# Scale and shift of the normalised rows ahead of the feed-forward: on VectorE in pieces, in place of GpSimd

## The chip, the core and the metric

The kernel runs on one core of a Trainium2 chip. The metric is the device time of one execution in microseconds. The core's engines work side by side, each through its own queue in order: TensorE (PE; PEld is its weight load), VectorE (DVE), ScalarE (ACT), GpSimd (POOL), and SyncE (SP), whose queue starts the transfers (DMA).

## What is computed

A decoder trunk of two layers over 256 tokens of 2048 values, float32. Cut to what matters here, of each layer:

```python
mod = (silu(c) @ w_ada[l] + b_ada[l]).reshape(B, N_MOD, 1, D_MODEL)     # sh_m, sc_m, gt_m, sh_f, sc_f, gt_f
...                                                # attention and RWKV heads give mix
x = layer_norm(DEEPNORM_ALPHA * x + gt_m * mix, ln1_w[l], ln1_b[l])
u = x * (1 + sc_f) + sh_f
gate, up = jnp.split(u @ w_gate_up[l], 2, axis=-1)
ffn = (jax.nn.silu(gate) * up) @ w_down[l]
x = layer_norm(DEEPNORM_ALPHA * x + gt_f * ffn, ln2_w[l], ln2_b[l])
```

The first `layer_norm` ends with a scale by `ln1_w` and a shift by `ln1_b`. The change concerns these two operations.

## The kernel before

`channel` holds the second half of a layer. The rows after the output projection lie in `z` as two halves of 128 tokens with 2048 values each; `normalise` (L1069 to L1078) takes off the mean and divides by the deviation. From there two paths leave. On the first, `inputs` and `make_u` (L349 to L362) transpose `z` on TensorE in 128x128 blocks (L354, L1100), and ScalarE and VectorE make from each transposed column block the pair `u`, a rounded part and the remainder (L358, L360, L361; in layer 1 half of the blocks by L1105 to L1107). The scale and shift of the norm are folded into the factors `a` and `b` here, so that this path reads the unscaled `z`. On the second path `affine` (L1172 to L1181) multiplies `z` by `ln1_w` and adds `ln1_b`, in place, in 16 pairs of which each takes 512 columns of one half: 8 multiplications and 8 additions a layer, L1180 and L1181. Their result is read only when the down projection adds the residual (L1261). Since they write `z` in place, each has to come after the transposes that read its columns. The rows of `ln1_w` and `ln1_b` are loaded to all partitions (`lnw`, `lnb`, 1 MB each); the same two buffers are loaded again with `ln2_w` and `ln2_b` (L1233, L1235) once the last piece has read them.

The feed-forward goes through eleven gate steps f of 512 hidden columns. A gate step is one `stream` over 16 blocks of the contraction. For each block `steps` (L364 to L388) starts two transfers of 256 KB into `raw` (4 buffers), rounds them on ScalarE into `hi` (L380, 3 buffers), and takes the remainder on VectorE into `lo` (L381, 2 buffers); TensorE then runs 12 products of 128x512 (L402, L403, L405), of which L403 reads `lo`. Below, lo 8 and step 8 mean the eighth block of layer 0's first gate step.

Beside this a second stream computes the modulation `mod` from `w_ada`: a 512 KB transfer into `ast` (2 buffers) and one VectorE instruction into `aacc` (L257) for each part, about 1.1 per block while layer 0's first gate step runs and 0.75 after.

The order on each engine is not the order of the code: the Tile framework replays the program against its own timeline and places each instruction where it becomes ready there. The code's order sets only what may go before what. The same two operations stand behind the feed-forward for `ln2`, on VectorE already (L1275, L1276), between the u of the next layer.

Of the kernel before, what the change touches and what calls it, by code (L numbers as in the profile page):

```python
# [67 lines left out]
def hybrid_trunk_kernel(  # L68
# [8 lines left out]
    V, S, G, PE = nc.vector, nc.scalar, nc.gpsimd, nc.tensor  # L77
# [12 lines left out]
    def bank(name="mb", tag="mb"):  # L90

        if tag == "cb":
            return ps.tile([P, 512], F32, tag="cb", name=name)
        t = f"m{turn[0]}"
        turn[0] ^= turn[1]
        return ps.tile([P, 512], F32, tag=t, name=name, bufs=1)
# [293 lines left out]
    def stream(srcs, W, kts, lhs, pieces, banks, first=True, last=True, ts=(0, 1), room=None, held=None):  # L390


        kept = []
        for i, hi, lo in held or steps(srcs, W, kts, room):
            kept.append((i, hi, lo))
            lt = lhs[i]
            st, sp_ = first and i == 0, last and i == len(kts) - 1
            for t in ts:
                xh, xl = lt[:, 0, t * P:(t + 1) * P], lt[:, 1, t * P:(t + 1) * P]
                for q, (c0, w) in enumerate(pieces):  # L400
                    bt = banks[t][q][:, 0:w]
                    PE.matmul(bt, lhsT=xh, rhs=hi[:, c0:c0 + w], start=st, stop=False)  # L402
                    PE.matmul(bt, lhsT=xh, rhs=lo[:, c0:c0 + w], start=False, stop=False)  # L403
                for q, (c0, w) in enumerate(pieces):
                    PE.matmul(banks[t][q][:, 0:w], lhsT=xl, rhs=hi[:, c0:c0 + w], start=False, stop=sp_)  # L405
        return kept
# [21 lines left out]
    def all_banks(n, ts=(0, 1)):  # L428
        return {t: [next_bank() for _ in range(n)] for t in ts}
# [685 lines left out]
    def channel(l, ys, wa, fp):  # L1115
# [4 lines left out]
        def ht_tile():  # L1120
            return fp.tile([P, 2, 2 * T], F32R, tag="ht", name="ht", bufs=12)
# [18 lines left out]
        for o in (0, 512):  # L1140
            for t in range(2):
                zq = z[:, t, o:o + 512]
# [4 lines left out]
        for c0, w in ((1024, 512), (1536, 512)):  # L1147
# [7 lines left out]
            for ts in ((0,), (1,)) if apart else ((0, 1),):  # L1155
                if apart:
                    held = stream(src, w, kts[n:], ys[n:], pieces, bk, first=False, ts=ts, room=room_ht, held=held)
                for t in ts:
                    for q in range(nq):
                        o = c0 + q * 512  # L1160
                        zq = z[:, t, o:o + 512]
# [7 lines left out]
        parts = inputs(fp, z, l, "ln1_w", "ln1_b", l, 4, 3, us, SPLIT_F[l])  # L1169

        def affine():
            lw = fp.tile([P, D], F32, tag="lnw", name="lnw", bufs=2)  # L1172
            dma(lw, ln1_w[l:l + 1, :].to_broadcast([P, D]))
            lb = fp.tile([P, D], F32, tag="lnw", name="lnb", bufs=2)
            dma(lb, ln1_b[l:l + 1, :].to_broadcast([P, D]))
            for t in range(2):
                for q in range(4):
                    o = q * 512
                    zq = z[:, t, o:o + 512]
                    G.tensor_mul(zq, zq, lw[:, o:o + 512])  # L1180
                    G.tensor_add(zq, zq, lb[:, o:o + 512])  # L1181

        def finish(t):
            mv, rs = rstd(fp, stt[t])
# [11 lines left out]
        for lo_g, hi_g in ((0, 6), (6, 11)):  # L1196
            hts = []
            for f in range(lo_g, hi_g):
                def gu(rv, k0, m, f=f):
                    return [(rv[:, :, s * 512:(s + 1) * 512], wg[:, k0:k0 + m, s, f * 512:(f + 1) * 512]) for s in range(2)]  # L1200
                bk = all_banks(2)
                if f == 0:
                    held = None
                    for kts, ts in parts:
                        held = stream(gu, 1024, kts, us[kts[0]:], [(0, 512), (512, 512)], bk, kts[0] == 0, kts[-1] == KT - 1,
                                      ts, room_ht2 if ts == (0,) else None, held if ts == (1,) else None)
                    affine()
                    pace[0] = AF_[l]
                else:
                    stream(gu, 1024, list(range(KT)), us, [(0, 512), (512, 512)], bk)  # L1210
                hh = []
                for t in range(2):
                    sg = fp.tile([P, 512], F32, tag="sg", name="sg", bufs=2)
                    S.activation(sg, bk[t][0], AF.Silu)
                    V.tensor_mul(sg, sg, bk[t][1])
                    hh.append(sg)
                for k2 in range(2):
                    b = bank()
                    for i in range(2):
                        for t in range(2):  # L1220
                            PE.transpose(b[:, i * T + t * P:i * T + (t + 1) * P],  # L1221
                                         hh[t][:, (2 * k2 + i) * P:(2 * k2 + i + 1) * P], ident)
                    ht = ht_tile()
                    S.copy(ht[:, 0, :], b)
                    V.tensor_tensor(ht[:, 1, :], b, ht[:, 0, :].bitcast(F32), ALU.subtract)
                    for i in range(2):
                        hts.append(ht[:, :, i * T:(i + 1) * T])
            if first:
                gate_rows(gtf, l, 5)
            if not first:  # L1230
                stt = [fp.tile([P, 4, 6], F32, tag="bst", name="bst", bufs=2) for _ in range(2)]
                lw = fp.tile([P, D], F32, tag="lnw", name="lnw", bufs=2)
                dma(lw, ln2_w[l:l + 1, :].to_broadcast([P, D]))  # L1233
                lb = fp.tile([P, D], F32, tag="lnw", name="lnb", bufs=2)
                dma(lb, ln2_b[l:l + 1, :].to_broadcast([P, D]))  # L1235
            kts = list(range(4 * lo_g, 4 * hi_g))
            for c0, w in ((0, 1024), (1024, 512), (1536, 512)):
# [11 lines left out]
                for ts in ((0,), (1,)) if apart else ((0, 1),):  # L1249
# [5 lines left out]
                    for t in ts:  # L1255
                        for q in range(nq):
                            o = c0 + q * 512
                            zq = z[:, t, o:o + 512]
# [12 lines left out]
        for t in range(2):  # L1271
            for q in range(4):
                o = q * 512
                zq = z[:, t, o:o + 512]
# [73 lines left out]
```

## Time and profile before

| | |
|---|---|
| device time, median of 3 runs (lowest, highest) | 2716.19 us (2714.63, 2720.35) |
| profiled execution: device time, span of its core | 2716.41 us, 2714.6 us |
| busy share of TensorE, VectorE, ScalarE, GpSimd | 93%, 68%, 44%, 7% |
| transfers | 637.49 MB, mean 235 GB/s |
| L1180 and L1181 on GpSimd, 16 of each | 24.2 and 25.7 us |

A profile is read from the share of busy time to the stretches where the busiest engine waits: what it waits for there, and what that engine was doing. An instruction's row gives its start, its duration and, in brackets, how long its engine sat idle before it and what ended that. Where the row counts several instructions (x4), the duration is that of all.

### The profile page before, as it was taken

The numbers are of one execution on the slowest core, as the hardware profiler recorded it, in microseconds if no ns is written. First come the engines' busy times: TensorE is split into PE (matmuls) and PEld (weight loads), VectorE is DVE, ScalarE is ACT, GpSimd is POOL, SyncE is SP. The second block draws the span as 40 slices with busy tenths as digits, with TensorE's granted clock in tenths as the row PEclk, the third lists the DMA queues.
The fourth block names the chain that finished last, engine by engine and source line by source line (L and its number), as shares of the span: only waits on it lengthen the run. The fifth ranks groups of instructions, "written<-read, shape, count | busy, mean of one in ns | idle before, by whom it ended". The sixth has DMA issues, their size and how long they took to land. (4 is left out here: it accounts for less than half of the span.)

```text
span 2714.6 us, 41774 instructions
## 1 busy us (share of the span) xinstructions
PE 2517.3 (93%) x15325; PEld 2103.9 (78%) x15325; DVE 1853.5 (68%) x2437; ACT 1188.4 (44%) x2029; POOL 180.0 (7%) x387
## 2 busy tenths in 40 slices
PE   3789998797999999999999989989899999999998
PEld 2787886575788888888889877867788888888887
DVE  6877767879777777777788677565764545545456
ACT  2364452434444444444445544534444444344442
POOL 1002111003000000000000022110120000000000
PEclk9799997798999999999999999979999999999999
DMA  9968667597888888889888586423746655566654
GB/s 310 382 193 254 203 197 225 179 331 250 313 318 308 303 307 304 294 302 309 304 287 288 175 251 204 116 75 130 258 163 190 190 190 190 194 191 189 190 190 148
DMA packets 351999, 637.49 MB, mean 235 GB/s; under 512 B 75894, under 2 KB 142898, under 8 KB 350258
## 3 DMA queue, kind: packets, MB, share of 16 engines
q1 hardware_dynamic: 351794, 634.82, 71.1%
q8 instruction: 120, 1.97, 0.3%
q14 instruction: 85, 0.70, 0.1%
HBM read 622.08 MB, written 12.62 MB: 234 GB/s over the span
## 5 line engine op out<-in xcount | busy, mean ns | idle before, releaser
L380 ACT CAST hi<-raw 128x1024 fp32r<-128x1024 f32 (+2 forms) x728 | 757.8, 1044 | 1097.6 <-PE acc L405 810.6
L381 DVE TENSOR_TENSOR lo<-raw,hi 128x1024 fp32r<-128x1024 f32 (+2 forms) x728 | 885.9, 1220 | 515.8 <-PE acc L403 335.2
L403 PE MATMUL acc<-lo,u 128*128 128x512 f32 x1568 | 515.7, 396 | 16.9 <-DVE lo L381 16.6
L405 PE MATMUL acc<-hi,u 128*128 128x512 f32 x1568 | 507.3, 392 | 0.0
L257 DVE SCALAR_TENSOR_TENSOR aacc<-ast,cond,aacc 128x1024 f32<-128x1024 f32 x300 | 388.7, 1296 | 136.2 <-DMA ast<-in_w_ada_dram 135.1
L402 PE MATMUL acc<-hi,u 128*128 128x512 f32 x1568 | 459.7, 395 | 2.4 <-ACT u L360 1.1
L403 PEld LDWEIGHTS acc<-lo,u 128*128 128x128 f32 x1568 | 294.6, 189 | 83.9 <-DVE lo L381 23.7
L402 PEld LDWEIGHTS acc<-hi,u 128*128 128x128 f32 x1568 | 295.8, 189 | 65.4 <-ACT u L360 1.8
L405 PEld LDWEIGHTS acc<-hi,u 128*128 128x128 f32 x1568 | 296.4, 189 | 62.3 <-issue 0.7
L403 PE MATMUL acc<-lo,ht 128*128 128x512 f32 (+1 forms) x720 | 243.7, 377 | 2.7 <-DVE lo L381 2.6
L405 PE MATMUL acc<-hi,ht 128*128 128x512 f32 (+1 forms) x720 | 242.3, 375 | 0.0
L414 PE MATMUL acc<-u,hi 128*128 128x256 f32 x720 | 206.4, 293 | 12.9 <-ACT hi L380 12.9
L402 PE MATMUL acc<-hi,ht 128*128 128x512 f32 (+1 forms) x720 | 217.1, 376 | 0.0
L415 PE MATMUL acc<-u,hi 128*128 128x256 f32 x720 | 205.6, 292 | 0.0
L416 PE MATMUL acc<-u,lo 128*128 128x256 f32 x720 | 193.7, 295 | 5.3 <-DVE lo L381 5.3
L403 PEld LDWEIGHTS acc<-lo,ht 128*128 128x128 f32 x720 | 135.1, 188 | 28.8 <-DVE lo L381 5.2
L414 PEld LDWEIGHTS acc<-u,hi 128*128 128x128 f32 x720 | 142.8, 199 | 16.7 <-ACT hi L380 13.6
L405 PEld LDWEIGHTS acc<-hi,ht 128*128 128x128 f32 x720 | 135.6, 188 | 24.3
L402 PEld LDWEIGHTS acc<-hi,ht 128*128 128x128 f32 x720 | 134.8, 188 | 24.3
L415 PEld LDWEIGHTS acc<-u,hi 128*128 128x128 f32 x720 | 142.6, 198 | 3.5 <-issue 2.6
L416 PEld LDWEIGHTS acc<-u,lo 128*128 128x128 f32 x720 | 134.4, 198 | 9.5 <-DVE lo L381 6.9
L1067 POOL TENSOR_TENSOR brs<-brs,mhalf 128x1 f32<-128x1 f32 x8 | 5.2, 655 | 1637.3 <-DVE brs L1066 851.5
(349 smaller groups left out, 2950.9 us busy)
## 6 DMA issues: line engine op xcount, KB each, us to landing
ast<-in_w_ada_dram SPq DMA_DIRECT2D x368, 512.0 KB
raw<-in_w_gate_up_dram SPq DMA_DIRECT2D x704, 256.0 KB
raw<-in_w_down_dram SPq DMA_DIRECT2D x176, 512.0 KB
raw<-in_w_in_dram SPq DMA_DIRECT2D x82, 512.0 KB
raw<-in_w_out_dram SPq DMA_DIRECT2D x64, 512.0 KB
raw<-in_w_in_dram SPq DMA_DIRECT2D x120, 256.0 KB
ast<-in_w_ada_dram SPq DMA_DIRECT2D x32, 256.0 KB
lnw<-in_ln_w_dram SPq DMA_DIRECT2D x4, 1024.0 KB
```

The source lines that it names most:

```text
L257: ins = V.scalar_tensor_tensor(acc, t, cond[:, j:j + 1], acc, ALU.mult, ALU.add)
L380: S.copy(h, fl)
L381: ins = V.tensor_tensor(r, fl, h.bitcast(F32), ALU.subtract)
L402: PE.matmul(bt, lhsT=xh, rhs=hi[:, c0:c0 + w], start=st, stop=False)
L403: PE.matmul(bt, lhsT=xh, rhs=lo[:, c0:c0 + w], start=False, stop=False)
L405: PE.matmul(banks[t][q][:, 0:w], lhsT=xl, rhs=hi[:, c0:c0 + w], start=False, stop=sp_)
L414: PE.matmul(bt, lhsT=hi[:, c0:c0 + w], rhs=xh, start=st and opens, stop=False)
L415: PE.matmul(bt, lhsT=hi[:, c0:c0 + w], rhs=xl, start=False, stop=False)
L416: PE.matmul(bt, lhsT=lo[:, c0:c0 + w], rhs=xh, start=False, stop=sp_ and closes)
L1067: G.tensor_tensor(rs[:, 0:1], rs[:, 0:1], mhalf[:, 0:1], ALU.pow)
```

## The change

The multiplications and additions of `affine` are issued on VectorE. `affine` becomes a generator that hands control back after each pair; it is created after the first gate step, and two pairs are taken from it after the stream of each later gate step, so that in the code the last pair comes after the fifth gate step. Its two loads come with the first pair taken. Nothing else differs.

```diff
         def affine():
...
-                    G.tensor_mul(zq, zq, lw[:, o:o + 512])
-                    G.tensor_add(zq, zq, lb[:, o:o + 512])
+                    V.tensor_mul(zq, zq, lw[:, o:o + 512])
+                    V.tensor_add(zq, zq, lb[:, o:o + 512])
+                    yield
...
-                    affine()
+                    rows = affine()
                     pace[0] = AF_[l]
                 else:
                     stream(gu, 1024, list(range(KT)), us, [(0, 512), (512, 512)], bk)
+                    for _ in range(2):
+                        next(rows, None)
```

The framework does not leave the pieces where the code has them. In layer 0, VectorE's queue from the end of the normalisation (L1078) into the first gate step has this order before:

```order
L1078 TENSOR_SCALAR z<-z,brs 128x512 x2
L257 SCALAR_TENSOR_TENSOR aacc<-ast,cond,aacc 128x1024
L361 TENSOR_TENSOR u<-uf,u 128x256 x4
L381 TENSOR_TENSOR lo<-raw,hi 128x1024
L257 SCALAR_TENSOR_TENSOR aacc<-ast,cond,aacc 128x1024
L361 TENSOR_TENSOR u<-uf,u 128x256 x2
```

and, from the same place on, this one after the change (the multiplication is L1181 there and the addition L1182):

```order
L1078 TENSOR_SCALAR z<-z,brs 128x512 x2
L257 SCALAR_TENSOR_TENSOR aacc<-ast,cond,aacc 128x1024
L1181 TENSOR_TENSOR z<-z,lnw 128x512 x2
L361 TENSOR_TENSOR u<-uf,u 128x256
L1182 TENSOR_TENSOR z<-z,lnb 128x512 x2
L361 TENSOR_TENSOR u<-uf,u 128x256 x2
L381 TENSOR_TENSOR lo<-raw,hi 128x1024
L257 SCALAR_TENSOR_TENSOR aacc<-ast,cond,aacc 128x1024
L361 TENSOR_TENSOR u<-uf,u 128x256 x2
```

All 16 pieces stand among the u and lo of the first gate step, in four groups like this one, one for each 512 columns, as GpSimd's did; and a lo has up to three u and one aacc fewer ahead of it than before. Layer 1 has the same, among L1105, L1107 and L361.

In SyncE's queue the reload of the two buffers with the rows of ln2 has moved behind one more pair of weight transfers. This is the piece of the queue before:

```order
L372 DMA raw<-in_w_gate_up_dram 128x512 x2
L1233 DMA lnw<-in_ln_w_dram 128x2048
L253 DMA ast<-in_w_ada_dram 128x1024
L372 DMA raw<-in_w_gate_up_dram 128x512 x2
L1235 DMA lnb<-in_ln_b_dram 128x2048
```

and this is it after; the two loads are L1237 and L1239 there and wait for VectorE's last pieces:

```order
L372 DMA raw<-in_w_gate_up_dram 128x512 x2
L253 DMA ast<-in_w_ada_dram 128x1024
L372 DMA raw<-in_w_gate_up_dram 128x512 x2
L1237 DMA lnw<-in_ln_w_dram 128x2048
L253 DMA ast<-in_w_ada_dram 128x1024
L372 DMA raw<-in_w_gate_up_dram 128x512 x2
L1239 DMA lnb<-in_ln_b_dram 128x2048
```

The transfers are the same ones; the pair of weights for step 13 now starts ahead of `lnw`.

At one other place the order differs by more than single rows: in the attention of layer 1, VectorE takes the rotation of the queries (qr) and the end of a block inverse (tm, ytr) ahead of a softmax division and not behind it:

```order
+L757 TENSOR_TENSOR tm<-tm,m_17427 128x512
+L898 TENSOR_TENSOR qr<-ra,rb 128x5x32
+L899 TENSOR_TENSOR qr<-ra,rb 128x5x32
+L745 STREAM_TRANSPOSE ytr<-tm 128x512
+L898 TENSOR_TENSOR qr<-ra,rb 128x5x32
+L899 TENSOR_TENSOR qr<-ra,rb 128x5x32
 L948 TENSOR_TENSOR den<-den,es 128x8
 L949 RECIPROCAL den<-den 128x8
```

The six instructions stood behind the division (L954) before; the neighbouring parts of that attention block are shuffled likewise on TensorE and ScalarE.

## Rows read from the trace of the kernel before

**Rows 1.** The page's first part: busy time of each engine, share, count.

```profile
PE 2517.3 (93%) x15325; PEld 2103.9 (78%) x15325; DVE 1853.5 (68%) x2437; ACT 1188.4 (44%) x2029; POOL 180.0 (7%) x387
```

**Rows 2.** Stretches: length, busy per engine, clock, DMA share, GB/s.

```profile
core 0: us, PE busy (x) PEld busy (x) DVE busy (x) ACT busy (x) POOL busy (x), PEclk, DMA share, GB/s
...
640.00:700.00 60.00, 41.32 (x172) 32.49 (x173) 53.71 (x49) 29.67 (x61) 27.47 (x17) 0.83 0.66 210
...
700.00:750.00 50.00, 49.18 (x219) 39.65 (x218) 37.47 (x34) 22.30 (x25) 0.00 (x0) 1.00 0.94 330
...
sum 700.00, PE 694.70 PEld 572.85 DVE 529.64 ACT 308.50 POOL 0.00; mean PE 49.62 PEld 40.92 DVE 37.83 ACT 22.04 POOL 0.00
...
1425.00:1455.00 30.00, 29.41 (x234) 28.38 (x233) 28.18 (x43) 23.12 (x40) 0.00 (x0) 0.93 0.69 226
...
1975.00:1980.00 5.00, 5.00 (x25) 4.17 (x24) 4.88 (x11) 3.11 (x8) 2.71 (x2) 1.00 0.00 0
```

**Rows 3.** VectorE in order of time, layer 0's first gate step: start, duration, instruction.

```profile
651.96 5.71 DVE L361 TENSOR_TENSOR u<-uf,u 128x256 fp32r<-128x256 f32 x4
657.59 1.21 DVE L381 TENSOR_TENSOR lo<-raw,hi 128x1024 fp32r<-128x1024 f32 x1
658.73 1.27 DVE L257 SCALAR_TENSOR_TENSOR aacc<-ast,cond,aacc 128x1024 f32<-128x1024 f32 x1
659.92 2.94 DVE L361 TENSOR_TENSOR u<-uf,u 128x256 fp32r<-128x256 f32 x2
662.78 2.30 DVE L381 TENSOR_TENSOR lo<-raw,hi 128x1024 fp32r<-128x1024 f32 x1
...
667.24 0.75 DVE L361 TENSOR_TENSOR u<-uf,u 128x256 fp32r<-128x256 f32 x2
...
685.19 2.28 DVE L381 TENSOR_TENSOR lo<-raw,hi 128x1024 fp32r<-128x1024 f32 x1
```

**Rows 4.** GpSimd in order of time, same stretch, its last two pieces.

```profile
682.74 3.64 POOL L1181 TENSOR_TENSOR z<-z,lnb 128x512 f32<-128x512 f32 x2
```

**Rows 5.** GpSimd's first line of the pieces: shortest, median, longest in ns.

```profile
L1180 POOL TENSOR_TENSOR z<-z,lnw x16: 1263/1468/2264, 651.4 to 1999.5; 128x512 f32<-128x512 f32 x16
```

**Rows 6.** Waits by total, 636 to 760 us: us, times, longest.

```profile
PE acc L403 <- DVE lo L381: 8.6, 5, 4.3
POOL z L1180 <- PE mb L354: 8.0, 3, 3.9
```

**Rows 7.** TensorE in order of time, layer 0's first gate step.

```profile
687.52 0.74 PE L403 MATMUL acc<-lo,u 128*128 128x512 f32 x2 [4.25 <-DVE lo L381]
...
698.34 0.61 PE L403 MATMUL acc<-lo,u 128*128 128x512 f32 x2
...
701.06 0.61 PE L403 MATMUL acc<-lo,u 128*128 128x512 f32 x2
...
712.59 1.52 PE L402 MATMUL acc<-hi,u 128*128 128x512 f32 x6
```

**Rows 8.** VectorE at the same operation behind layer 0's feed-forward, in order of time.

```profile
1425.10 1.29 DVE L1275 TENSOR_TENSOR z<-z,lnw 128x512 f32<-128x512 f32 x2 [0.96 <-PE mb L354]
1426.31 0.42 DVE L361 TENSOR_TENSOR u<-uf,u 128x256 fp32r<-128x256 f32 x1
```

**Rows 9.** SyncE's queue of transfers in order of time, layer 0's first gate step.

```profile
687.54 0.81 SPq L372 DMA_DIRECT2D raw<-in_w_gate_up_dram  x2
...
692.84 0.63 SPq L1235 DMA_DIRECT2D lnb<-in_ln_b_dram  x1
```

**Rows 10.** ScalarE in order of time, layer 0's first gate step.

```profile
709.27 1.06 ACT L380 CAST hi<-raw 128x1024 fp32r<-128x1024 f32 x1 [1.47 <-DMA raw<-in_w_gate_up_dram]
```

**Rows 11.** ScalarE in order of time, start of layer 1's first gate step.

```profile
1962.38 1.04 ACT L380 CAST hi<-raw 128x1024 fp32r<-128x1024 f32 x1 [3.35 <-DMA raw<-in_w_gate_up_dram]
```

**Rows 12.** VectorE in order of time, attention of layer 1.

```profile
1823.48 0.17 DVE L948 TENSOR_TENSOR den<-den,es 128x8 f32<-128x8 f32 x1 [3.24 <-ACT pr L947]
...
1827.30 0.70 DVE L745 STREAM_TRANSPOSE ytr<-tm 128x512 f32<-128x512 f32 x1
```

## The prediction

> **What bounds the kernel now.** TensorE is busy for 93% of the span, VectorE for 68%, GpSimd for 7% [rows 1], so I looked first for stretches in which TensorE is not full. Around the work that the change moves there is one: in the 60 us from 640 on TensorE has 41.32 us at a mean clock of 0.83, VectorE 53.71 and GpSimd 27.47 [rows 2]. After 700 TensorE is full again: 694.70 of 700 us up to 1400, with the transfers at a share of 0.94 in the first 50 us [rows 2]. Whatever makes layer 0's first gate step end earlier is therefore carried on by a full TensorE; nothing behind it waits for a fixed time.
>
> VectorE in order of time comes next [rows 3]. From 651.96 up to lo 8 at 685.19 no row has an idle time: VectorE is the limit here, and TensorE waits 8.6 us for `lo` (once 4.25, at step 8) [rows 6, 7]. The rows also show two prices for one instruction. Two u in a row take 0.75 us where GpSimd is idle and 2.94 where it runs; a lo 1.21 and 2.30 [rows 3]. From start to start an undisturbed lo takes 1.14 and an aacc 1.19 (657.59, 658.73, 659.92), and a u 0.34 (half of 0.75, less the 0.07 by which each runs into the next); a stretched one of any size takes about 1.07 more, much the same for an instruction of 0.34 as for one of 1.19. That is a wait, not a slower pace: GpSimd's 16 pieces (the last two end at 686.38 [rows 4]) each hold up one VectorE instruction. I count 16 stretched instructions in this step of layer 0, 15 of them ahead of lo 8. The count can be checked: from 651.96 to lo 8 VectorE has 13 u, 5 lo and 6 aacc, 4.42 + 5.70 + 7.14 = 17.3 us, and 15 x 1.07 = 16.0; 651.96 + 33.3 = 685.3, and lo 8 starts at 685.19 [rows 3].
>
> GpSimd's instruction itself takes 1.263 us at best and up to 2.264 [rows 5], so the delay runs both ways. The Trainium skill (SBUF — State Buffer, Who interferes with whom) calls what the two engines share an exclusive lock: an instruction with two inputs in SBUF and a GpSimd instruction that reads SBUF exclude each other, and the later one waits for the whole of the first. By that rule a stretch could be as long as GpSimd's 1.263, and the removal worth 20.2 in place of the 17.1 below; the trace agrees in kind, and its 1.07 is what I use.
>
> **The change part by part, layer 0.** Removed: 16 stretches of 1.07 us, 17.1 us of VectorE's queue. Added: 16 instructions of 128x512. The trace has the same operation on VectorE behind the feed-forward: two in 1.21 us from start to start [rows 8], 0.605 each, so 9.7 us. The difference is 7.4 us up to the last u.
>
> The new order adds to it, since fewer u and aacc stand ahead of each lo. Walked with the same prices, VectorE has ahead of lo 8 now 10 u, 5 lo, 5 aacc and 12 pieces: 3.40 + 5.70 + 5.95 + 7.26 = 22.3, so lo 8 starts at 674.3, 10.9 earlier. From there to lo 12 come 4 lo, 6 u, 3 aacc and the last 4 pieces: 4.56 + 2.04 + 3.57 + 2.42 = 12.6; lo 12 ends at 688.0. TensorE begins L403 of step 12 at 701.06 now [rows 7]. It could follow: from step 8 at 675.4, four steps of 2.72 us (its spacing where it is full, 698.34 to 701.06 [rows 7]) bring it to 686.3. So step 12 starts 13.1 us earlier. The pieces' new wait, for the transposes that read their columns, I cost at nothing: the twin operation waits 0.96 us once, for the same transposes [rows 8], and TensorE has 29.41 of 30 us there while VectorE has 28.18 [rows 2]. The other bound is rival three. What is queued behind a waiting piece is the next u and lo, and TensorE behind that lo.
>
> Next late are the transfers. Before, the cast of step 16 waited for its weights and began at 709.27 [rows 10], 21.7 us after the weights of step 12 were started at 687.54 [rows 9]. These are started when lo 8 is done, now at 675.4. If the same burst again takes 21.7 us, step 16 is there at 697.1. The load of `lnb` started 5.3 us after those weights at 692.84 [rows 9]; now it waits for VectorE's last piece, at 683.9 in the walk, 8.5 after, and holds the queue with the weights of steps 15 and 16 for up to 3.2 us more: 700.3, and with the cast 701.4. TensorE's own pace gives 698.9 (step 12's first product at 687.1, four steps, an allowance of 0.9 for transposes). Step 16 began at 712.59 [rows 7]; it gains 11.2 to 13.7. I take 12.0, nearer to the transfers' limit, which ends last in this walk.
>
> **Layer 1 and the attention.** In layer 1's first gate step the pieces stretch VectorE as well, but TensorE is full there: 5.00 of 5 us at 1975 with GpSimd at 2.71 [rows 2]; and its start is set by a transfer, the cast at 1962.38 that waited 3.35 us for weights [rows 11]. I take 0, between -1 and +1. In the attention of layer 1 VectorE idles 3.24 us before the division at 1823.48, and the transpose at 1827.30 came after it [rows 12]. The new order can start that transpose up to 3 us sooner, or put the six instructions, some 2.2 us, ahead of the division. I take 0, and keep -3 to +2 for the range.
>
> GpSimd's other work loses its neighbour in the queue; nothing waited for it there. Sum: 2716.41 - 12.0 = 2704.4 for the profiled execution, which lies 0.2 us above the median of the runs; forecast 2704.
>
> **The rivals.** One, VectorE's own sum alone: the order is worth nothing, because the u and aacc that now come later are wanted as soon as the lo. Then 7.4 us go: 2709. The check of the sum speaks for the prices; against this rival, TensorE waited for `lo` and never for an aacc.
>
> Two, the transfers give it all back: they had a share of 0.66 in 640 to 700 [rows 2], and if the weights can't come sooner for a reason that this trace doesn't show (two loads of 1 MB among them), step 16 stays near 712 and the time at 2713 to 2717. Against it: the queue waited for buffers that VectorE frees, not for the engines of the transfers.
>
> Three, slower: VectorE takes over GpSimd's waits. GpSimd sat 8.0 us in front of its pieces waiting for transposes, 3.9 at most [rows 6], with nothing behind it; VectorE in the same place holds u and lo, and these transposes wait for banks that the u have to free. 9.7 + 8.0 - 17.1 = +0.6, and with three waits of 3.9 it is 9.7 + 11.7 - 17.1 = +4.3: 2717 to 2721. It decides from 7.4 us of such waits on. Against it: the twin's single 0.96.
>
> Four, slower too: the stretched instructions have some other cause (the transposes, the loads), and a saturated VectorE simply gets 9.7 us more: 2726. The count of 16 for 16 and the undisturbed rows between the pieces speak against it. The Trainium skill (Perfetto Trace Analysis, Optimizing Scalar/DVE Operations) advises for a saturated VectorE to move work off it, even to GpSimd; the same place warns that the two share a read port. By the advice alone this change goes the wrong way, and the price is the one just given.
>
> **How the numbers follow.** The forecast, 2701 to 2707, has 0.58; rival one, 2707 to 2711, 0.18; rival two 0.13; rival three 0.06; rival four 0.05. A measurement of this kernel can tell about 0.2%, 5.4 us, from no change. Faster by more than that: nearly all of the forecast, 0.56, most of rival one, 0.15, and 0.02 of rival two, 0.73. Slower: half of rival three and rival four, with 0.01 for the attention, 0.09. The rest, 0.18, is within. The range takes in the forecast with 3 us for the attention and 3 for the gate step below it, rival one and the nearer part of rival two: 2698 to 2714.
>
> **What would show it.** In the profile after, no u, lo or aacc of the first gate steps is stretched; the 16 pieces of layer 0 take 0.69 us each with at most 2 us of idle time ahead of them in all; lo 8 starts about 11 us earlier after the same start of the step; TensorE has no wait over 1 us for `lo`; the product at 712.59 comes near 700.5. An L403 of step 12 near 694 would show rival one. A cast that waits several us for weights past step 13 would show rival two, waits for L354 in front of L1181 rival three, stretched rows without GpSimd rival four. The forecast is wrong if TensorE, once ahead, is stopped again before 1400.

## The result, and the profile of the changed kernel

The changed kernel takes 2698.58 us in the median (six runs) against 2716.48 for the kernel before in the runs beside it: a ratio of 0.9939, with a 95% interval from 0.9923 to 0.9954. That is faster by about 17 us (12 to 21). Forecast were 2704, and 2698 to 2714. Its profiled execution has a span of 2697.1 us against 2714.6.

The page's first part, which answers to [rows 1]: VectorE has 32 instructions more and is nevertheless busy for 10 us less (1853.5 before).

```profile
PE 2507.4 (93%) x15325; PEld 2097.6 (78%) x15325; DVE 1843.0 (68%) x2469; ACT 1189.2 (44%) x2029; POOL 132.2 (5%) x355
```

Stretches, as in [rows 2]: length, busy time of each engine, clock, DMA share, GB/s. In the 60 us from 640 TensorE is busy for 50.83 us and not 41.32, at a clock of 0.90 and not 0.83.

```profile
640.00:700.00 60.00, 50.83 (x232) 41.47 (x233) 53.31 (x71) 36.06 (x67) 0.55 (x1) 0.90 0.83 287
680.00:690.00 10.00, 9.53 (x46) 7.96 (x47) 9.12 (x12) 4.49 (x14) 0.00 (x0) 1.00 0.99 399
700.00:750.00 50.00, 50.00 (x227) 41.41 (x226) 39.77 (x37) 21.39 (x24) 0.00 (x0) 1.00 0.95 340
```

VectorE in order of time in layer 0's first gate step, as [rows 3]: start, duration, instruction. No row is stretched: a u takes 0.34 from start to start, a lo 1.14, a piece (L1181, L1182) 0.60, and no row has an idle time ahead of it that a piece caused.

```profile
649.73 1.28 DVE L1181 TENSOR_TENSOR z<-z,lnw 128x512 f32<-128x512 f32 x2
650.93 0.42 DVE L361 TENSOR_TENSOR u<-uf,u 128x256 fp32r<-128x256 f32 x1
651.26 1.29 DVE L1182 TENSOR_TENSOR z<-z,lnb 128x512 f32<-128x512 f32 x2
...
653.22 1.23 DVE L381 TENSOR_TENSOR lo<-raw,hi 128x1024 fp32r<-128x1024 f32 x1
654.36 1.28 DVE L257 SCALAR_TENSOR_TENSOR aacc<-ast,cond,aacc 128x1024 f32<-128x1024 f32 x1
...
672.32 1.22 DVE L381 TENSOR_TENSOR lo<-raw,hi 128x1024 fp32r<-128x1024 f32 x1
...
680.66 1.29 DVE L1182 TENSOR_TENSOR z<-z,lnb 128x512 f32<-128x512 f32 x2
```

TensorE's wait for `lo` from 636 to 760, which was 8.6 us in five pieces [rows 6], and its rows that answer to [rows 7]; step 12 begins with L403 at 686.86 and step 16 with L402 at 697.08.

```profile
PE acc L403 <- DVE lo L381: 0.8, 1, 0.8
```

```profile
686.07 1.03 PE L277 MATMUL mb<-ident,aacc 128*128 128x128 f32 x8
686.86 0.71 PE L403 MATMUL acc<-lo,u 128*128 128x512 f32 x2
...
697.08 1.07 PE L402 MATMUL acc<-hi,u 128*128 128x512 f32 x4
```

SyncE's queue as [rows 9] (the weights of step 12, and `lnb`) and ScalarE as [rows 10]: the second cast is that of step 16, and it waits for TensorE to give a buffer back, not for weights. The cast of step 14 did wait for weights, 3.96 us, but early enough to stop nobody.

```profile
673.57 0.81 SPq L372 DMA_DIRECT2D raw<-in_w_gate_up_dram  x2
...
681.99 0.33 SPq L1239 DMA_DIRECT2D lnb<-in_ln_b_dram  x1
```

```profile
687.64 1.06 ACT L380 CAST hi<-raw 128x1024 fp32r<-128x1024 f32 x1 [3.96 <-DMA raw<-in_w_gate_up_dram]
...
694.41 1.05 ACT L380 CAST hi<-raw 128x1024 fp32r<-128x1024 f32 x1 [1.45 <-PE acc L405]
```

Where the time went is read from stretches that begin and end at the same instructions in both kernels. The first fence is before, the second after. In each, the first line runs from layer 0's first gate product to the first product of its down projection, the other two from layer 1's first gate product over the start of its second half (the columns behind the first eight blocks) to its down projection.

```profile
651.98:941.93 289.95, 279.88 (x1251) 228.78 (x1251) 223.35 (x202) 137.06 (x214) 26.37 (x16) 0.98 0.86 297
1963.67:1990.59 26.92, 26.24 (x113) 21.40 (x113) 17.52 (x39) 10.53 (x24) 7.80 (x7) 0.91 0.32 102
1990.59:2236.74 246.15, 245.63 (x1104) 203.00 (x1105) 129.44 (x116) 110.15 (x124) 11.55 (x8) 1.00 0.61 193
```

```profile
649.92:927.45 277.53, 275.30 (x1251) 226.47 (x1251) 217.12 (x219) 137.26 (x214) 0.00 (x0) 1.00 0.89 311
1948.11:1974.65 26.54, 26.54 (x116) 21.40 (x117) 18.61 (x47) 11.45 (x26) 0.73 (x1) 0.91 0.31 101
1974.65:2219.27 244.62, 244.62 (x1103) 202.70 (x1102) 125.59 (x122) 109.21 (x122) 0.00 (x0) 1.00 0.61 194
```

Layer 0's stretch is 12.4 us shorter. TensorE's idle time in it fell from 10.1 to 2.2 us (the length less PE busy), and its busy time for the same 1251 matmuls from 279.9 to 275.3, because between the waits of before it was at times granted the lower of its two clocks (0.66 in the mean of the 5 us from 686.98; 0.98 over the stretch, against 1.00 after). Layer 1's two stretches are 1.9 us shorter. Two differences remain: the first gate product of layer 0 begins at 649.92 in place of 651.98, and the attention of layer 1 takes 83.06 us in place of 86.25; the input projection ahead of that attention takes 2.6 more. The experiments tell which of these belong to the change.

### The profile page after: what moved, and what is told of

Same layout as the page of the kernel before. It is cut to its first block, busy times and chain, and to the rows that moved or that the text cites. A ratio compares the mean times of both kernels' runs of the same rounds, so it can differ in the third digit from the quotient of the medians.

```text
span 2697.1 us, 41748 instructions
## 1 busy us (share of the span) xinstructions
PE 2507.4 (93%) x15325; PEld 2097.6 (78%) x15325; DVE 1843.0 (68%) x2469; ACT 1189.2 (44%) x2029; POOL 132.2 (5%) x355
## 4 chain that ended last, share of the span: by engine, by line
PE 74%; DMA 12%; DVE 8%; issue 2%; POOL 2%; ACT 1%; SPq 1%; DVEq 0%; POOLq 0%; ACTq 0%
PE acc L403 19%; PE acc L405 19%; PE acc L402 19%; DMA ast<-in_w_ada_dram 7%; PE acc L416 3%; PE acc L415 3%; PE acc L414 3%; DVE lo L381 2%; DVE aacc L257 2%; DMA raw<-in_w_in_dram 1%; DMA raw<-in_w_gate_up_dram 1%; POOL tmp L733 1%; DMA raw<-in_w_out_dram 1%; PE aa L684 1%; PE mb L1225 1%
## 5 line engine op out<-in xcount | busy, mean ns | idle before, releaser
L403 PE MATMUL acc<-lo,u 128*128 128x512 f32 x1568 | 513.0, 394 | 9.2 <-DVE lo L381 9.2
L402 PE MATMUL acc<-hi,u 128*128 128x512 f32 x1568 | 458.0, 393 | 0.5 <-ACT u L360 0.5
L403 PEld LDWEIGHTS acc<-lo,u 128*128 128x128 f32 x1568 | 294.0, 189 | 74.2 <-DVE lo L381 13.4
L402 PEld LDWEIGHTS acc<-hi,u 128*128 128x128 f32 x1568 | 295.0, 189 | 62.2 <-ACT u L360 0.9
L403 PE MATMUL acc<-lo,ht 128*128 128x512 f32 (+1 forms) x720 | 243.6, 377 | 2.7 <-DVE lo L381 2.6
L414 PE MATMUL acc<-u,hi 128*128 128x256 f32 x720 | 207.9, 295 | 13.1 <-ACT hi L380 13.1
L402 PE MATMUL acc<-hi,ht 128*128 128x512 f32 (+1 forms) x720 | 217.0, 376 | 0.0
L403 PEld LDWEIGHTS acc<-lo,ht 128*128 128x128 f32 x720 | 135.0, 188 | 29.2 <-DVE lo L381 5.5
L402 PEld LDWEIGHTS acc<-hi,ht 128*128 128x128 f32 x720 | 134.8, 188 | 24.4
```

The lines of the kernel that those rows point to most:

```text
L414: PE.matmul(bt, lhsT=hi[:, c0:c0 + w], rhs=xh, start=st and opens, stop=False)
```

## The experiments

Eleven kernels were run, each timed beside the kernel before. The table gives the length of stretches in each profile, in us: "out" is from the first product of layer 0's output projection to its first gate product, "gate 0" and "gate 1" are the stretches above, "in 1" is the input projection of layer 1 from its first product to the end of its last, and "att 1" the attention from there to the first product of the output projection.

| kernel | ratio to before (95%) | out | gate 0 | in 1 | att 1 | gate 1 |
|---|---|---|---|---|---|---|
| before | | 121.1 | 289.95 | 348.2 | 86.25 | 273.07 |
| changed | 0.9939 (0.9923, 0.9954) | 119.3 | 277.53 | 350.8 | 83.06 | 271.16 |
| 1 layer 0 only | 0.9947 (0.9935, 0.9959) | 119.9 | 278.53 | 352.8 | 84.35 | 273.58 |
| 2 layer 1 only | 0.9996 (0.9985, 1.0007) | 122.1 | 291.01 | 351.6 | 85.95 | 270.98 |
| 3 pieces on GpSimd | 0.9995 (0.9986, 1.0005) | 120.4 | 289.93 | 349.7 | 86.11 | 273.19 |
| 4 both engines | 0.9976 (0.9966, 0.9985) | 120.2 | 289.08 | 350.7 | 87.75 | 270.59 |
| 5 VectorE late | 0.9953 (0.9936, 0.9971) | 118.7 | 278.07 | 348.8 | 86.17 | 272.95 |
| 6 GpSimd late | 0.9956 (0.9939, 0.9973) | 110.1 | 281.79 | 350.2 | 83.44 | 277.49 |
| 7 VectorE at once | 0.9951 (0.9933, 0.9969) | 119.3 | 278.26 | 351.0 | 83.08 | 271.09 |
| 8 copies and memsets | 0.9950 (0.9934, 0.9967) | 119.4 | 278.24 | 348.8 | 83.52 | 270.74 |
| 9 rows late | 0.9908 (0.9890, 0.9925) | 109.4 | 278.59 | 349.8 | 82.74 | 270.98 |
| 10 rows late, not bound | 0.9935 (0.9920, 0.9950) | 111.8 | 282.72 | 348.1 | 89.17 | 270.44 |
| 11 changed, again | 0.9946 (0.9930, 0.9962) | 118.9 | 279.02 | 349.4 | 83.71 | 270.94 |

### 1 and 2: one layer at a time

VectorE takes the pieces of one layer, GpSimd those of the other (layer 0 on VectorE here; the second kernel has `l == 1`):

```diff
-                    V.tensor_mul(zq, zq, lw[:, o:o + 512])
-                    V.tensor_add(zq, zq, lb[:, o:o + 512])
+                    E = V if l == 0 else G
+                    E.tensor_mul(zq, zq, lw[:, o:o + 512])
+                    E.tensor_add(zq, zq, lb[:, o:o + 512])
                     yield
...
                     rows = affine()
+                    if l != 0:
+                        list(rows)
```

> VectorE does the pieces in layer 0 only; layer 1 keeps them on GpSimd. The profile after the change puts 13.7 us of the gain into layer 0's first gate step, 3.2 into the attention of layer 1, and about 2 into the end of layer 1's first gate step. In this kernel the order of layer 1's attention is that of the changed kernel. Theory (the stretches in layer 0 and the order of the attention pay): 2716.5 - 13 - 3 = about 2700. Rival A (the attention's 3.2 us is scatter between two executions): about 2703 to 2704. Rival B (layer 1's own pieces carry as much as the 5 us beyond my sum): 2703 or more, with the attention at its shorter length.

Measured: 2701.90 us; gate 0 278.53, gate 1 273.58, the attention 84.35.

> VectorE does the pieces in layer 1 only; layer 0 keeps them on GpSimd, and the attention of layer 1 keeps the order of before. Theory (layer 1's first gate step is full on TensorE, so its pieces are worth 0 to 2 us): 2714.5 to 2716.5, and layer 0's first 290 us as long as before. Rival (layer 1's pieces carry the 5 us that my sum lacks): about 2711.5.

Measured: 2715.05 us; gate 0 291.01, gate 1 270.98.

Layer 0 brings most of the gain by itself, layer 1 little: its interval reaches from 0.9985 to 1.0007. The two stretches keep to their own edit: gate 0 is short only where layer 0's pieces left GpSimd, gate 1 only where layer 1's did. My rival B for the first kernel, and the rival for the second, fall: layer 1 does not carry 5 us. By the profiles its stretch carries 2.3. The time of the first kernel lies between the theory (2700) and rival A (2703 to 2704) and does not tell them apart.

### 3 and 7: is it the pieces, or the engine

One kernel keeps GpSimd and hands the pieces out after later steps, the other has VectorE and issues all at once. The framework makes of the first the same sequence on every engine as that of before, and of the second that of the changed kernel. So the part of the change that its name speaks of, the pieces between later gate steps, does nothing, and each is a second execution of a known kernel.

```diff
-                    V.tensor_mul(zq, zq, lw[:, o:o + 512])
-                    V.tensor_add(zq, zq, lb[:, o:o + 512])
+                    G.tensor_mul(zq, zq, lw[:, o:o + 512])
+                    G.tensor_add(zq, zq, lb[:, o:o + 512])
                     yield
```

> The pieces are handed out two after each later gate step as in the change, but stay on GpSimd. The framework gives every engine the same sequence of instructions as before. Theory (the engine alone matters, and cutting into pieces is nothing): 2716.5, same as before within 0.1%, so that this is a second profiled execution of the kernel before: each stage's length within 1 us or so of the first one's tells how much of a difference between two profiles is scatter. Rival (the pieces bring part of the gain by something that the order doesn't show, the loads' dependencies for one): 2705 to 2712.

Measured: 2714.64 us; gate 0 289.93, gate 1 273.19, the attention 86.11.

```diff
                     rows = affine()
+                    list(rows)
```

> The pieces on VectorE, but issued all at once behind the first gate step as before. The framework gives every engine the same sequence of instructions as in the changed kernel. Theory (the pieces between later steps are nothing): 2699 to 2701, a second profiled execution of the changed kernel: layer 0's stretch 277 to 279 us, layer 1's 271 to 272. Its attention tells whether the 83.06 us there are the order's: 83 to 85 if they are, 86 to 88 if they go with the granted clock, as in the kernel with both engines at work, which had the same order and 87.75 us at a clock of 0.66 in one of its 15 us. Rival (pieces matter): 2705 or more.

Measured: 2701.83 us; gate 0 278.26, gate 1 271.09, the attention 83.08.

Gate 0 and gate 1 repeat within 0.8 us in these two pairs (a third execution of the changed kernel, number 11, has 1.5 us more in gate 0). "Out" and "in 1" spread more: over the profiles in which nothing there was changed by 3.4 and 4.7 us. Up to VectorE's first piece at 649.73 every queue has the same order before and after in "out". So I take the 2.06 us ahead of the first gate product and the 2.6 in the input projection for scatter between two executions, of opposite sign, and for no effect of the change.

### 4: both engines at work

The changed kernel, and GpSimd multiplies beside it, in layer 0 only, into a buffer that nobody reads. All other queues are the changed kernel's.

```diff
                     rows = affine()
+                    if l == 0:
+                        scr = fp.tile([P, 512], F32, tag="scr", name="scr")
+                        for kt in range(KT):
+                            uv = us[kt].rearrange("p a t -> p (a t)").bitcast(F32)
+                            G.tensor_mul(scr, uv, uv)
```

> The changed kernel, and beside it 16 multiplications of 128x512 on GpSimd in layer 0's first gate step, each from a u that has just been made into a buffer that nobody reads; the queues of all other engines are those of the changed kernel. Theory (a GpSimd instruction holds up one VectorE instruction by about 1.07 us each): 17.1 us more of VectorE's queue in a step that leaves it about 2 us of slack, so the gate step 13 to 17 us longer than after the change, 2711 to 2716, the u, lo and aacc stretched again in the number of GpSimd's instructions. Rival (what paid was VectorE's order, with fewer u and aacc ahead of each lo, or the wait of the pieces): 2698 to 2700, no stretched rows.

Measured: 2711.19 us; gate 0 289.08. GpSimd, then VectorE in the same stretch, in order of time:

```profile
652.43 1.36 POOL L1214 TENSOR_TENSOR scr<-u 128x512 f32<-128x512 f32 x1 [5.74 <-DVE u L361]
654.82 3.07 POOL L1214 TENSOR_TENSOR scr<-u 128x512 f32<-128x512 f32 x2 [1.03 <-DVE u L361]
```

```profile
651.88 0.42 DVE L361 TENSOR_TENSOR u<-uf,u 128x256 fp32r<-128x256 f32 x1
652.21 2.13 DVE L1182 TENSOR_TENSOR z<-z,lnb 128x512 f32<-128x512 f32 x2
...
654.94 2.06 DVE L381 TENSOR_TENSOR lo<-raw,hi 128x1024 fp32r<-128x1024 f32 x1
```

An undisturbed u takes 0.42. The u, the pieces, the lo and the aacc that ran into a multiplication take 0.85 more than their 0.41, 1.28 (for two), 1.21 and 1.27. I count 16 stretched rows for GpSimd's 16 instructions, 13.6 us of VectorE's queue; TensorE waits for `lo` again, and gate 0 is 10.7 us longer than the mean 278.3 of the kernels with these queues (changed, 1, 7, 11):

```profile
PE acc L403 <- DVE lo L381: 9.5, 6, 2.7
```

```profile
651.02:940.10 289.08, 278.41 (x1251) 227.43 (x1251) 229.61 (x219) 136.76 (x214) 26.78 (x16) 0.99 0.86 299
```

So GpSimd's work beside VectorE is by itself worth nearly all that the change gained in layer 0. The rival that only the order paid falls, and with it the order of the loads in SyncE's queue, which is that of the changed kernel here. The order of VectorE's queue may be worth something too: VectorE is busy for 229.61 us in this stretch against 223.35 before, and it is still 0.9 us shorter. That is argued from the sums; no kernel changes the order alone, and the multiplications reach on to 700 us, where GpSimd was done at 686.4 before. The size was over-estimated: the multiplication of one tensor with itself stretches by 0.85, not by 1.07 as the pieces did.

### 5 and 6: the pieces behind the first gate step

On VectorE, with each pair bound behind the last lo of the step after which the code has it:

```diff
-                    V.tensor_mul(zq, zq, lw[:, o:o + 512])
+                    ins = V.tensor_mul(zq, zq, lw[:, o:o + 512])
+                    tc.add_manual_dep(ins.ins, anchor[0], order, reason="after this gate step")
```

> VectorE's pieces are bound behind the last lo of the gate step after which the code puts them, so none is left in the first gate steps. There VectorE has neither GpSimd's stretches nor the 9.7 us of pieces. The order of layer 1's attention is that of before. Theory (after the change the first gate step is already at TensorE's own pace: it waits 0.79 us once): layer 0 from the first product of the gate steps to the first of the down projection 276 to 278 us, against 277.5 after the change and 289.9 before; layer 1's first two stretches 271 as after the change; the attention 86 as before; so 2716.4 - 12.5 - 2.4 = 2701 to 2702. Rival (VectorE still held the first gate step): 274 us or less there, 2697 to 2699. Rival (the pieces cost later, where VectorE is busy for 75% with the weights and the modulation): 280 us or more, 2704 or more.

Measured: 2704.48 us; gate 0 278.07, gate 1 272.95, the attention 86.17.

Gate 0 is as expected: taking the 9.7 us of pieces out of the first step brings nothing more, since VectorE no longer sets its pace. Gate 1 is not (271 was expected, and with it a time of 2701 to 2702): it has 272.95, as before the change, though neither engine has a piece in that step. So what layer 1 won is not GpSimd's absence. TensorE's queue shows what it is. The three fences are before, after, and this kernel: transposes (L354) and the first product of the second half.

```profile
1988.88 1.04 PE L354 MATMUL mb<-ident,z 128*128 128x128 f32 x8
1990.59 0.50 PE L402 MATMUL acc<-hi,u 128*128 128x512 f32 x1 [0.68 <-ACT u L360]
```

```profile
1963.36 0.49 PE L354 MATMUL mb<-ident,z 128*128 128x128 f32 x3
...
1967.36 0.27 PE L354 MATMUL mb<-ident,z 128*128 128x128 f32 x1
...
1973.86 1.04 PE L354 MATMUL mb<-ident,z 128*128 128x128 f32 x8
```

```profile
1968.68 1.03 PE L354 MATMUL mb<-ident,z 128*128 128x128 f32 x8
1970.39 0.50 PE L402 MATMUL acc<-hi,u 128*128 128x512 f32 x1 [0.68 <-ACT u L360]
```

In the changed kernel the framework has put four of the sixteen transposes 7 to 11 us ahead of that product, which starts at 1974.65, while TensorE is still in the first half; the first u are there in time, and the wait of 0.68 us is gone. In this kernel (the last fence) the eight transposes stand right in front of it, as before, and the wait is there. That is an effect of the planning, which moved with the engine of the pieces. It explains 0.68 of the 2.4 us; before, another 0.5 stood at 2016 (a product behind the gate's activation), gone as well; the rest lies in TensorE's busy time, and I have not taken it apart.

On GpSimd, with the rows of the norm loaded behind the weights of the second gate step, so that the pieces can't start sooner:

```diff
-                    affine()
...
                     stream(gu, 1024, list(range(KT)), us, [(0, 512), (512, 512)], bk)
+                    if f == 1:
+                        affine()
...
-            dma(lw, ln1_w[l:l + 1, :].to_broadcast([P, D]))
+            ins = dma(lw, ln1_w[l:l + 1, :].to_broadcast([P, D]))
+            tc.add_manual_dep(ins.ins, load[0], order, reason="behind gate step 1")
```

> The pieces stay on GpSimd, all at once, but their two rows are loaded behind the weights of the second gate step, so that they run from there on. Theory (a GpSimd piece costs only where VectorE is what TensorE waits for): VectorE has 37.5 of 50 us after 700, so 17 us of stretches find about 12 us of room and TensorE loses 0 to 5; layer 0's stretch 277 to 282 us against 289.9, layer 1's 271 to 272; 2702 to 2707. Rival (a stretch costs TensorE wherever it lies): 288 us or more, 2714 or more.

Measured: 2702.12 us; gate 0 281.79, gate 1 277.49. The 30 us of layer 0's stretch in which GpSimd works:

```profile
727.02:757.02 30.00, 27.21 (x124) 21.07 (x122) 20.84 (x16) 14.13 (x30) 29.43 (x16) 1.00 0.68 264
```

Theory held for layer 0: TensorE is idle for 2.8 us of these 30, and gate 0 is 8.2 us shorter than before without one piece on VectorE. Layer 1 missed by 5 us, and not through VectorE: behind the late loads the casts waited for weights (us, times, longest, 2020 to 2070), which no cast does at the same place before:

```profile
ACT hi L381 <- DMA raw<-in_w_gate_up_dram: 20.2, 7, 7.8
```

The surprise is "out": 110.1 us, where no piece was ever placed. The time met its range by luck, since the miss in layer 1 and this gain cancel in part.

### 8: what GpSimd must do to stand in the way

```diff
                     rows = affine()
+                    if l == 0:
+                        scr = fp.tile([P, 512], F32, tag="scr", name="scr")
+                        for kt in range(0, KT, 2):
+                            uv = us[kt].rearrange("p a t -> p (a t)").bitcast(F32)
+                            G.tensor_copy(scr, uv)
+                            G.memset(scr, 0.0)
```

> The changed kernel, and beside it on GpSimd in layer 0's first gate step 8 copies of 128x512 from a u and, behind each, one memset of 128x512. The queues of the other engines are those of the changed kernel. Theory A (any GpSimd instruction that touches SBUF holds up VectorE's): 16 stretched VectorE rows, the layer 0 stretch 287 to 290 us, 2709 to 2712. Theory B (the Trainium skill, SBUF - State Buffer, Who interferes with whom: what excludes the other is a GpSimd instruction that reads SBUF): 8 stretched rows beside the copies and none beside the memsets; at 0.85 to 1.07 us each 7 to 9 us of VectorE's queue, less its slack of 2: 282 to 286 us, 2704 to 2707. Theory C (only GpSimd's instructions with two operands do it): none, 277 to 279 us, 2699 to 2701.

Measured: 2704.16 us; gate 0 278.24. GpSimd, then VectorE, in order of time:

```profile
673.34 1.53 POOL L1214 COPY scr<-u 128x512 f32<-128x512 f32 x1 [3.30 <-DVE u L361]
674.93 0.53 POOL L1215 MEMSET scr<- 128x512 f32 x1
677.96 5.68 POOL L1214 COPY scr<-u 128x512 f32<-128x512 f32 x1 [2.50 <-DVE u L361]
```

```profile
674.33 0.82 DVE L361 TENSOR_TENSOR u<-uf,u 128x256 fp32r<-128x256 f32 x1
675.08 1.21 DVE L381 TENSOR_TENSOR lo<-raw,hi 128x1024 fp32r<-128x1024 f32 x1
...
683.09 1.63 DVE L257 SCALAR_TENSOR_TENSOR aacc<-ast,cond,aacc 128x1024 f32<-128x1024 f32 x1
```

Eight VectorE rows are stretched, each beside one of the eight copies (the u at 674.33 takes 0.82 and not 0.41, the aacc at 683.09 1.63 and not 1.27). Of the memsets two have a row to themselves, the lo at 675.08 and one at 685.39, and these are not stretched; the other six fall into a row beside their copy, which is no longer than the rest of its kind. That is theory B in kind. The Trainium skill (SBUF — State Buffer, Who interferes with whom) says just that: a GpSimd instruction that only writes does not contend. The size I had wrong: I had carried over the 0.85 to 1.07 us of the multiplications and the pieces, and VectorE loses 0.35 to 0.41 us beside a copy that takes 0.90 alone. Eight times that is 3 us, and gate 0, for which theory B had 282 to 286, is no longer than without: VectorE has that much room in this step. The time does not tell the theories apart here (2693.76 to 2714.45 in ten runs). GpSimd waits too, and longer: the copy at 677.96 took 5.68 us, while VectorE ran six instructions past it.

### 9 to 11: the rows of the norm out of the output projection

"Out" in kernel 6 pointed to the two loads of 1 MB that the pieces need. Before, SyncE starts them amid the output projection's weights:

```profile
565.95 0.60 SPq L1173 DMA_DIRECT2D lnw<-in_ln_w_dram  x1
```

Kernel 9 keeps layer 1 as the change has it, and in layer 0 binds VectorE's pieces as kernel 5 does and the loads as kernel 6 does:

```diff
             ins = dma(lw, ln1_w[l:l + 1, :].to_broadcast([P, D]))
+            if l == 0:
+                tc.add_manual_dep(ins.ins, load[0], order, reason="behind gate step 1")
...
-                    V.tensor_mul(zq, zq, lw[:, o:o + 512])
+                    ins = V.tensor_mul(zq, zq, lw[:, o:o + 512])
+                    if l == 0:
+                        tc.add_manual_dep(ins.ins, anchor[0], order, reason="after this gate step")
```

> Layer 0's pieces on VectorE, each pair bound behind the last lo of its later gate step, and the two loads of 1 MB that they read bound behind the weights of the second gate step. Layer 1 as in the changed kernel. Reason: in the kernel with GpSimd late, which bound the same loads, the time from the output projection's first product to layer 0's first gate product was 110.1 us, against 118.7 to 122.1 in eight kernels that load these rows at about 566 us, amid the output projection's weights. Theory (the two loads hold up the weights there): 109 to 111 us again; layer 0's stretch 278 to 280, layer 1's first two 271 to 272; 2690 to 2693, ahead of the changed kernel by 8. Rival (the earlier start is given back, since the loads now hold up the weights of the second gate step): layer 0's stretch 286 or more, 2698 or more. Rival (the 110.1 was scatter): 118 to 122 us, 2699 to 2702.

Measured: 2689.07 us, ratio 0.9908; "out" 109.38, gate 0 278.59, gate 1 270.98. The loads in its queue:

```profile
717.25 0.56 SPq L1175 DMA_DIRECT2D lnw<-in_ln_w_dram  x1
```

And the output projection from its first product to the end of its last, first in the changed kernel (number 11), then here:

```profile
524.59:628.87 104.28, 95.31 (x415) 75.13 (x414) 82.98 (x103) 41.85 (x79) 1.21 (x2) 0.98 0.92 329
```

```profile
527.24:626.46 99.22, 94.57 (x415) 74.39 (x414) 82.76 (x102) 42.04 (x79) 0.00 (x0) 0.99 0.92 323
```

The products take 5.1 us less, of which 4.3 were idle time of TensorE, with the transfers at the same share (99.2 to 101.8 us in kernels 6, 9 and 10, 103.6 to 106.6 in the profiles with the early loads). That is what the theory says, and the loads' cost is not paid again in the second gate step. But it is only about half of the 9.5 us by which "out" is shorter. The other 4.5 lie between the last of these products and the first gate product. Here are VectorE's aacc in that time alone (length, TensorE, its weight loads, VectorE), in the same two kernels:

```profile
628.87:643.50 14.63, 0.00 (x0) 0.00 (x0) 7.62 (x6) 0.66 0.71 220
```

```profile
626.47:636.62 10.15, 0.00 (x0) 0.00 (x0) 3.32 (x3) 0.72 0.66 217
```

In the changed kernel, as before, six aacc stand there among the instructions of the normalisation, and VectorE waits 3.0 to 3.4 us for their transfers; in kernels 6, 9 and 10 the framework has put three there, and the waits are 0.8 to 1.0. So moving the two loads gave the whole, but half of it came through another order in VectorE's queue. No kernel takes the two apart.

> The same loads bound behind the weights of the second gate step in layer 0, the pieces on VectorE but not bound: the framework places all 16 in one run as soon as the rows are there. Theory: the output projection 109 to 111 us as in the kernel before this one; VectorE has 75% of its time taken in the second gate step, 16 pieces of 0.605 us are 9.7 us in some 30 us of it, so TensorE waits 0 to 4 us: layer 0's stretch 278 to 282, 2690 to 2695. Rival (pieces cost nothing wherever they are, since TensorE is full): no difference to the bound ones, within 0.1%.

Measured: 2696.52 us, ratio 0.9935; "out" 111.8, gate 0 282.72. Here the pieces are not bound (the second edit of kernel 9 is left out), and the framework puts them into VectorE's queue almost in one run, from 724.75 to 736.8 with a single lo among them. TensorE pays with one wait, and the time is above the 2690 to 2695 expected:

```profile
737.99 1.22 PE L404 MATMUL acc<-lo,u 128*128 128x512 f32 x2 [4.31 <-DVE lo L382]
```

> The changed kernel itself on the same chip, to hold the two kernels with late loads against. 2698 to 2702; from the output projection's first product to the first gate product 118 to 121 us, layer 0's stretch 277 to 279, layer 1's 271 to 272. Its attention is one more sample: theory (its order avoids the fall of the clock behind the first 55 us): 83 to 84.5 us; rival (chance): 86 or more.

Measured: 2700.52 us, ratio 0.9946; "out" 118.9, gate 0 279.02, gate 1 270.94, the attention 83.71. On the same chip kernel 9 is 11 us faster than the changed kernel, with intervals of the ratio that do not meet (0.9890 to 0.9925, 0.9930 to 0.9962): it beats both.

## Why the prediction was right, and where its terms were off

**The stretches: right.** One VectorE instruction held up for each of GpSimd's, the reason for the whole forecast, is shown by kernel 4, which brings 16 of them back and with them 10.7 us.

**VectorE's walk: right to 0.1 us.** Lo 8 was to start at 674.3 for a step that starts at 651.98; the step started 2.06 earlier, and lo 8 at 672.32. The pieces at 0.605 each and their wait at nothing held as well: no wait in front of a piece in layer 0; in layer 1 one of 4.27 us that TensorE never felt. Rival three (VectorE takes over GpSimd's waits) had no part.

**Step 12: 1 us late.** It starts 12.1 us sooner, the 2.06 taken off, in place of 13.1: eight transposes of the modulation (L277, at 686.07) stood ahead of its L403, which I had not carried along.

**Step 16 and the transfers: the wrong end ended last.** I chose 12.0 out of 11.2 to 13.7, near the transfers' limit. It gained 13.5, near TensorE's own pace. The step that failed is "if the same burst again takes 21.7 us": the weights of step 12 were started at 673.57 and the cast of step 16 ran at 694.41, held by a buffer and not by weights. From 680 to 690 the transfers moved 399 GB/s. That 12.0 was nevertheless what layer 0 brought over the whole stretch (12.4 in the first pair, 12.0 between the means of before, 2 and 3 and of changed, 1, 7 and 11) is partly luck: TensorE gave the rest back in short waits for `lo` between 769 and 785.

**The rivals.** One, the order worth nothing, gave 7.4 us for layer 0; 12.0 were measured, and the sums of kernel 4 speak for a share of the order. Two, the transfers, fell with the 399 GB/s; its sign, a cast behind step 13 that waits several us for weights, was there once (3.96, step 14), but TensorE waited for no cast. Four, another cause of the stretches, fell with kernel 4: they come and go with GpSimd's reading instructions.

**Layer 1: mis-sized.** I took 0, between -1 and +1, from 5 us in which TensorE was full. It gave 2.4 us (273.3 as the mean of before, 1 and 3, against 270.9 as that of the eight profiles with VectorE among that step's pieces). What I said of contention there was right: without any of it kernel 5 has 272.95. What I had not read is TensorE's own wait of 0.68 at the start of the second half, and that the planning would move transposes.

**Attention: not settled.** The 3.2 us of the first pair were outside my -3 by a little, and kernels 1, 7, 8 and 11, with the same order, have 83.1 to 84.4. But kernel 4 has that order too and takes 87.75, and with the order of before the seven profiles spread from 82.74 (kernel 9) to 89.17 (kernel 10). What goes with the length is TensorE's clock. Here are stretches of 5 us from 50 us into the attention on: two of before, two of after, and the second one of kernel 9, whose order there is that of before:

```profile
1823.93:1828.93 5.00, 3.17 (x48) 2.71 (x50) 5.00 (x20) 1.40 (x4) 0.29 (x1) 0.97 0.00 0
1828.93:1833.93 5.00, 5.00 (x47) 4.33 (x46) 3.34 (x19) 1.23 (x3) 0.00 (x0) 0.50 0.02 5
```

```profile
1812.13:1817.13 5.00, 4.30 (x76) 3.76 (x78) 4.93 (x20) 0.84 (x3) 0.29 (x1) 1.00 0.02 5
1817.13:1822.13 5.00, 5.00 (x43) 3.48 (x39) 2.77 (x17) 2.27 (x10) 0.00 (x0) 1.00 0.10 32
```

```profile
1804.00:1809.00 5.00, 5.00 (x52) 3.20 (x50) 3.29 (x16) 3.34 (x14) 0.00 (x0) 1.00 0.00 0
```

Before, TensorE was busy for 3.17 of the first 5 us, and then granted 0.50, the lower of its two levels (1.2 GHz of 2.4); after, it was busy for 4.30, and kept 1.00, as in kernel 9. In the six profiles in which 0.50 is granted there or within 15 us behind, the attention takes 85.9 us or more, in the seven others 84.4 or less. The size fits as well: kernel 10 was granted 0.51, 0.50 and 0.62 in the three such stretches from 55 us on, which by an estimate cost 6.9 us of the full clock (5 x (0.49 + 0.50 + 0.38)), and its attention is 6.4 longer than that of kernel 9, with the same order. Whether the order changes the odds of that is open; six and seven profiles don't tell it.

So the gain is 12.0 in layer 0, which is what the forecast counted, and 2.4 in layer 1, which it did not: 14.4 us. The rest of the 17 in the first comparison I put down to the attention's clock and to scatter. The three timings of this sequence of instructions (changed, 7, 11) say 16.6, 13.3 and 14.7 us.

## What to carry to other kernels

Whether two engines hold each other up is read from the durations of equal instructions: if one takes 1.2 us in one place and 2.3 in another, count the stretched ones against the other engine's instructions before pricing a move. Moving work onto the busier engine can pay where each piece costs it less than the disturbance did (0.605 against 1.07), and moving it out of the step that is tight pays as well, on either engine. And look at what the moved work loads: here starting its two loads later gave some 9 us, nearly as much as the contention had cost, about half of it where they had stood among other transfers and half through the order that the framework then chose.

## What the runs showed of the hardware

- The time that VectorE loses to one GpSimd instruction of 128x512 differs with the instruction: 1.07 us for a piece with two tensors that takes 1.26 at its shortest, 0.85 for the product of one tensor with itself (1.36), 0.35 to 0.41 for a copy (0.90), and nothing for the two memsets (0.53) that had a row to themselves.
- The loss is not even: in these steps no VectorE instruction was held for longer than that, and a GpSimd copy once for nearly 5 us (5.68 in place of 0.90).
- TensorE's granted clock in the attention of layer 1 differs between executions with the same order of instructions there, and the length goes with it: 82.74 us at 1.00 throughout those stretches (kernel 9), 89.17 with three at 0.50 to 0.62 (kernel 10).
